# Moving one layer's conditioning dots out of the feed-forward stages and regrouping two feed-forward stages

## The chip, the cores and the metric

The kernel runs on one core of a Trainium2 chip. The metric is the device time of one launch in microseconds (us), the median over runs. A core has five engines that run their own queues: TensorE (PE, matmuls, with PEld for its weight loads), VectorE (DVE), ScalarE (ACT), GpSimd (POOL), and SyncE (SP), which here issues nearly all DMA transfers. They wait for each other through semaphores.

## What is computed

A trunk of two layers over 256 latent tokens and 256 context tokens of width 1024. Every sublayer is normalised, shifted, scaled and gated by vectors that come from a conditioning vector (one for the latent stream, one for the context stream):

```python
for l in range(DEPTH):
    mx = split(silu(c)     @ ada_w[l] + ada_b[l], 9)      # latent stream
    mc = split(silu(c_ctx) @ ada_w[l] + ada_b[l], 9)      # context stream
    x  = x  + mx[2]*0.5*swiglu(modulate(x,  gain[l,0], mx[0], mx[1]), ffn1[l])
    xc = xc + mc[2]*0.5*swiglu(modulate(xc, gain[l,0], mc[0], mc[1]), ffn1[l])
    y_x, y_c = token_mixer(modulate(x, gain[l,1], mx[3], mx[4]),
                           modulate(xc, gain[l,1], mc[3], mc[4]), ...)
    x  = x + mx[5]*y_x
    x  = x + mx[8]*0.5*swiglu(modulate(x, gain[l,2], mx[6], mx[7]), ffn2[l])
    # context likewise, except in the last layer, which drops it after the mixer
return rmsnorm(x) * final_norm
```

`swiglu(h) = (silu(h @ w1) * (h @ w3)) @ w2` with an inner width of 2816, that is 22 tiles of 128. The mixer has three branches (latent attention, differential attention, retention), each gated and summed.

## The kernel before

**Order of the work.** Start-up (norm and the first three inner tiles), FFN (0,0), mixer of layer 0, FFN (0,1), FFN (1,0), mixer of layer 1, FFN (1,1), final norm. PE's instructions stand in the order in which the program writes them; the other engines' instructions and the buffers are ordered by the framework's scheduler, which goes by program order among what it believes to be ready. An order that it has fixed does not change on the chip: an engine waits for the head of its queue.

**Weights.** Every matmul is done in three with a value cut into a high and a low part. `unit` (L193) loads 128 x 1024 weights (512 KB) through SP into one of four `raw` buffers (pool `rawp`), and cuts them in pieces of `PIECE` = 256 columns: ACT copies the high part (`whi`, L206), DVE subtracts it for the low part (`wlo`, L207). Four such cut pairs can exist (pool `wp`). A unit narrower than 1024 is cut in one piece.

**Large tiles.** Pool `qkv` has 16 buffers ("pair") of 512 KB, for inner tiles `g`, the forms `tf`, and all larger tiles of the mixer.

**FFN.** `ffn` (L606) makes the 22 inner tiles in `FF_GROUPS` of 8, 8 and 6. After each group `out_phase` (L404) multiplies them by w2 for 8 output chunks c and adds each chunk into x by DVE (`evac`, L412, two halves of 256 columns). Matmuls of the out phase go chunk by chunk, except that with `nfirst` = 2 the first two chunks go together, inner tile by inner tile. PSUM has three `mm` banks for them.

**Strassen FFNs.** (0,1) and (1,0) make inner tiles in pairs by seven products of half-size blocks instead of eight (`ff_pairs`, L545, `product` of 24 matmuls of 256 columns). The products of a pair come in the order b21, n2, n1, n3, b11 of the next pair (`begin`), n4, b22. `block` (L525) loads a block of weights; with `plus` POOL adds a second one in by an accumulating DMA (W2+W3 for `n`, W0+W2 for `r3`). `cut_weight` (L518) cuts it: ACT L521, then DVE L522. `n` is also added to `r0` (L570), which is then cut for the product n2. One `mm` bank belongs to the pair that has begun, also across an out phase. `token_forms` builds the six `tf` tiles first.

**Conditioning dots.** For a modulation vector m and a chunk k of 128 rows, `ada` (L284) loads 128 x 1024 of `ada_w` (512 KB, tile `araw`, SP L292), and `ada_dot` (L278) multiplies and sums it with silu(c) of each stream on DVE (L281). Each 128-row chunk is a load and one dot for each stream that needs it. `hook(n)` (L309) allows 2n dots more and writes them at that place in the program; `PACE` = (per inner step, per output chunk) sets n. In FFN (0,0) the dots are those of layer 0 (vectors 2 to 8) and of layer 1 (vectors 0 to 2): 80 loads, 160 dots, at PACE (3.2, 1.5). FFN (0,1) has vectors 3 and 4 of layer 1 (16 loads, 32 dots), FFN (1,0) vectors 5 to 8 for the latent stream alone (32 loads, 32 dots), both at one `hook(1.0)` for each chunk of an out phase that is not the last. `cond` (L269) loads c and c_ctx and applies Silu.

**Mixer.** It calls `gemm` (L223) 89 times in layer 0, in this order of what matters here: 8 for differential attention's q and k, 8 for retention and 2 for the latent k/v as fill between the steps of differential attention, then a gate (8 x 3 matmuls) and a projection (4 x 3) alternately for the second and the third branch, with 6 for the latent branch's q and rotary parts in between, then the heads. Every call takes one weight unit or half of one.

## Time and profile before

| what | us |
|---|---|
| median of 3 runs (2298.07 to 2298.66) | 2298.34 |
| the profiled execution's own time | 2294.51 |
| its span, first to last instruction | 2292.6 |
| PE busy | 2207.6 |
| DVE busy | 1621.8 |
| ACT busy | 1058.1 |
| moved by DMA | 345.44 MB, mean 151 GB/s |

The span is the time that the profile shows; the profiled execution's own time is 1.9 us more. PE's busy time is modelled, so a stretch is also judged by how many matmuls of which width it holds against a stretch in which PE never waits. Busy time of the other engines is a union of instructions, and two that follow each other closely overlap by some tens of ns.

### The profile page before, as it was taken

What the parts mean: (1) busy time and instruction counts of PE and PEld (TensorE: products, weight loads), DVE (VectorE), ACT (ScalarE), POOL (GpSimd) and SP (SyncE); (2) the same over time, 40 slices, a digit from 0 to 9 for tenths busy, and PEclk for the clock granted to TensorE, in tenths of its full rate; (3) what the DMA queues carried; (4) which work ended last, traced back from release to release, by engine and by line L of the source; (5) the groups of instructions that cost most, each with busy time, mean ns of one, the idle gap of its engine ahead of it and who ended that gap; (6) DMA issues with size and microseconds to landing.
All of it is one profiled execution on the core that took longest, in us unless ns stands there. A gap on an engine that the chain in (4) does not pass through costs nothing.

```text
span 2292.6 us, 36217 instructions
## 1 busy us (share of the span) xinstructions
PE 2207.6 (96%) x13578; PEld 1933.6 (84%) x13578; DVE 1621.8 (71%) x3604; ACT 1058.1 (46%) x2617; POOL 131.8 (6%) x166
## 2 busy tenths in 40 slices
PE   9989989999999999999999998989999999999998
PEld 6868777887788877898898998888988889989998
DVE  4899998658645455678875776777567786777665
ACT  4413223437533256444353545335354574565554
POOL 2000000000000000000000000000000000110000
PEclk9999999999999999999999999999999999999999
DMA  8567665331213313436764635885452233435553
GB/s 316 193 220 230 228 209 193 122 101 56 74 54 97 94 61 96 140 93 199 219 174 119 176 79 152 268 248 173 127 176 91 96 111 116 152 117 178 185 184 111
DMA packets 98271, 345.44 MB, mean 151 GB/s; under 512 B 11312, under 2 KB 12208, under 8 KB 98096
## 3 DMA queue, kind: packets, MB, share of 16 engines
q1 hardware_dynamic: 89568, 313.76, 41.6%
q0 software_dynamic: 7808, 27.27, 6.1%
q8 instruction: 107, 1.75, 0.3%
q10 hardware_dynamic: 720, 2.11, 0.3%
q14 instruction: 68, 0.56, 0.1%
HBM read 338.89 MB, written 4.19 MB: 150 GB/s over the span
## 4 chain that ended last, share of the span: by engine, by line
PE 60%; DVE 16%; issue 11%; DMA 11%; ACT 2%; POOL 0%; POOLq 0%; DVEq 0%; SPq 0%; ACTq 0%
PE mm L216 15%; PE mm L217 15%; PE mm L218 14%; DVE junk L281 7%; DMA raw<-in_w13p 5%; DMA araw<-in_ada 5%; DVE wlo L522 2%; DVE wlo L207 2%; PE s L216 2%; PE s L217 2%; PE s L218 2%; PE o L211 2%; PE s L211 2%; PE t L211 2%; PE t L912 1%
## 5 line engine op out<-in xcount | busy, mean ns | idle before, releaser
L206 ACT CAST whi<-raw 128x256 fp32r<-128x256 f32 (+1 forms) x1222 | 437.9, 421 | 391.7 <-PE mm L218 139.1
L207 DVE TENSOR_TENSOR wlo<-raw,whi 128x256 fp32r<-128x256 f32 x1214 | 481.8, 440 | 185.0 <-ACT whi L206 183.1
L216 PE MATMUL mm<-h,wlo 128*128 128x256 f32 (+2 forms) x1272 | 435.4, 342 | 0.4 <-DVE wlo L207 0.4
L218 PE MATMUL mm<-h,whi 128*128 128x256 f32 (+2 forms) x1272 | 426.3, 335 | 0.0
L217 PE MATMUL mm<-h,whi 128*128 128x256 f32 (+2 forms) x1272 | 426.0, 335 | 0.0
L216 PE MATMUL mm<-g,wlo 128*128 128x512 f32 (+1 forms) x758 | 269.5, 355 | 25.0 <-DVE wlo L207 20.1
L281 DVE SCALAR_TENSOR_TENSOR junk<-araw,cond 128x1024 bf16<-128x1024 f32 x224 | 271.6, 1218 | 22.7 <-DMA araw<-in_ada 22.3
L217 PE MATMUL mm<-g,whi 128*128 128x512 f32 (+1 forms) x758 | 266.7, 352 | 3.2 <-DVE g L601 1.7
L216 PEld LDWEIGHTS mm<-h,wlo 128*128 128x128 f32 (+1 forms) x1272 | 241.1, 190 | 33.2 <-issue 9.4
L218 PE MATMUL mm<-g,whi 128*128 128x512 f32 (+1 forms) x758 | 265.9, 351 | 0.0
L218 PEld LDWEIGHTS mm<-h,whi 128*128 128x128 f32 (+1 forms) x1272 | 240.9, 189 | 25.4
L217 PEld LDWEIGHTS mm<-h,whi 128*128 128x128 f32 (+1 forms) x1272 | 241.3, 190 | 22.4 <-issue 0.2
L216 PE MATMUL s<-h,wlo 128*128 128x256 f32 (+1 forms) x848 | 259.0, 305 | 0.0
L217 PE MATMUL s<-h,whi 128*128 128x256 f32 (+1 forms) x848 | 258.6, 305 | 0.0
L218 PE MATMUL s<-h,whi 128*128 128x256 f32 (+1 forms) x848 | 258.5, 305 | 0.0
L521 ACT CAST whi<-raw 128x1024 fp32r<-128x1024 f32 x140 | 145.5, 1047 | 162.3 <-DMA raw<-in_w13p 84.4
L522 DVE TENSOR_TENSOR wlo<-raw,whi 128x1024 fp32r<-128x1024 f32 x140 | 170.1, 1220 | 29.0 <-ACT whi L521 29.0
L216 PEld LDWEIGHTS mm<-g,wlo 128*128 128x128 f32 x758 | 144.1, 190 | 52.0 <-DVE wlo L207 19.9
L216 PE MATMUL mm<-tf,wlo 128*128 128x256 f32 x480 | 144.9, 302 | 35.9 <-DVE wlo L522 28.7
L216 PEld LDWEIGHTS s<-h,wlo 128*128 128x128 f32 x848 | 163.4, 193 | 6.8
L217 PEld LDWEIGHTS s<-h,whi 128*128 128x128 f32 x848 | 163.1, 192 | 6.7
L218 PEld LDWEIGHTS s<-h,whi 128*128 128x128 f32 x848 | 162.9, 192 | 6.7
(296 smaller groups left out, 3851.5 us busy)
## 6 DMA issues: line engine op xcount, KB each, us to landing
araw<-in_ada SPq DMA_DIRECT2D x128, 512.0 KB, 4.1
raw<-in_w13p SPq DMA_DIRECT2D x100, 512.0 KB, 3.5
raw<-in_w SPq DMA_DIRECT2D x90, 512.0 KB, 4.3
raw<-in_win SPq DMA_DIRECT2D x90, 512.0 KB, 3.5
raw<-in_w2a SPq DMA_DIRECT2D x64, 512.0 KB, 4.1
raw<-in_w13p POOLq DMA_DIRECT2D x40, 512.0 KB, 6.1
raw<-in_w2c SPq DMA_DIRECT2D x32, 384.0 KB, 3.1
raw<-in_wbr SPq DMA_DIRECT2D x24, 512.0 KB, 3.5
```

What stands on the lines that cost most here:

```text
L206: nc.scalar.copy(hi[:, c], raw[:, c])
L207: eng.tensor_tensor(out=lo[:, c], in0=raw[:, c], in1=hi[:, c].bitcast(F32), op=ALU.subtract)
L211: self.nc.tensor.matmul(out, lhsT=lhsT, rhs=rhs, start=start, stop=stop)
L216: nc.tensor.matmul(out, lhsT=sl, rhs=mh, start=start, stop=False, **kw)
L217: nc.tensor.matmul(out, lhsT=sh, rhs=ml, start=False, stop=False, **kw)
L218: nc.tensor.matmul(out, lhsT=sh, rhs=mh, start=False, stop=stop, **kw)
L281: self.nc.vector.scalar_tensor_tensor(out=junk, in0=raw, scalar=1.0, in1=cond[s], op0=ALU.mult, op1=ALU.mult, accum_out=self.mods[l][:, s, ...
L521: nc.scalar.copy(hi, raw)
L522: nc.vector.tensor_tensor(out=lo, in0=raw, in1=hi.bitcast(F32), op=ALU.subtract)
L912: nc.tensor.transpose(pt[:, b * 128:(b + 1) * 128], P[:, b * 128:(b + 1) * 128], self.ident)
```

## The change

All dots of layer 1 are written into the mixer of layer 0, at 1.8 dots for each `gemm` call (`DOTS` = 0.9), one stream after the other: 9 vectors for the latent stream (72 loads, 72 dots), then 5 for the context stream (40 loads, 40 dots). Each load now takes a `raw` buffer of `rawp`, the one that weights use; silu(c) takes one `qkv` buffer, loaded through POOL. FFN (0,0) keeps the 112 dots of layer 0 at PACE (2.2, 0.9). The Strassen FFNs have no dots, go in groups of 6, 6, 6 and 4 inner tiles with their own layout of w2 (`w2s`, `w2t`, made on the host as the other layouts are), and load `r1` and `n` of the next pair into `qkv` buffers when that pair begins. Groups of 6 start an out phase with two chunks together. Units of 1024 columns are cut in two pieces instead of four.

```diff
-PIECE = 256
+PIECE = 512
-PACE = ((3.2, 1.5), (0.0, 1.0), (0.0, 1.0))
+PACE = ((2.2, 0.9), (0, 0), (0, 0))
+ST_GROUPS = ((0, 6), (6, 12), (12, 18), (18, 22))
+DOTS = 0.9
...
     def gemm(self, out, w, acts, cols, m=128, off=0):
+        if self.mixing:
+            self.hook(DOTS)
...
+    def ada_streams(self, l, streams):
+        nc, a = self.nc, self.a
+        for s, mods in streams:
+            cond = self.qkv.tile([128, 1024], F32, tag="pair", name="cond1")
+            nc.gpsimd.dma_start(cond, a["cvec"][s].to_broadcast([128, 1024]))
+            nc.scalar.activation(cond, cond, AF.Silu)
+            for m in mods:
+                for k in range(KD):
+                    raw = self.rawp.tile([128, 1024], F32, tag="raw", name="araw")
+                    nc.sync.dma_start(raw, a["ada"][l, m, k])
+                    self.ada_dot(l, m, k, raw, {s: cond}, (s,))
+                    if k == KD - 1:
+                        self.ada_done(l, s, m)
+                    yield 1
...
-        nfirst = 2 if gm == 5 or len(halves) == 1 else 0
+        nfirst = 2 if gm == 5 or len(halves) == 1 or len(acts) == 6 else 0
...
-    def block(self, src, plus=None):
-        raw = self.rawp.tile([128, 1024], F32, tag="raw", name="raw")
+    def block(self, src, plus=None, pool=None):
+        if pool is None:
+            raw = self.rawp.tile([128, 1024], F32, tag="raw", name="raw")
+        else:
+            raw = pool.tile([128, 1024], F32, tag="pair", name="raw")
...
-            begun[p] = r0, q1, s1
+            n = self.block(W[p, 2], W[p, 3], pool=self.qkv)
+            r1 = self.block(W[p, 1], pool=self.qkv)
+            begun[p] = r0, r1, n, q1, s1
...
-            r1 = self.block(W[p, 1])
             q2, q3 = self.s_bank(), self.s_bank()
             self.product(q2, self.cut_weight(r1), B["b21"], True, True)
             add(out=s1, in0=s1, in1=q2, op=ALU.add)
             self.gated(s1, g1, HX)
-            n = self.block(W[p, 2], W[p, 3])
+            r3 = self.block(W[p, 0], W[p, 2])
             wn = self.cut_weight(n)
             add(out=r0, in0=r0, in1=n, op=ALU.add)
             self.product(q1, self.cut_weight(r0), B["n2"], False, False)
...
             self.product(q3, wn, B["n1"], True, False)
-            r3 = self.block(W[p, 0], W[p, 2])
+            r4 = self.block(W[p, 3])
...
             if p + 1 < NFF // 2:
                 begin(p + 1)
-            r4 = self.block(W[p, 3])
...
-        self.adaq = itertools.chain(self.ada(0, range(2, NMOD), cond), self.ada(1, range(3), cond))
+        self.adaq = self.ada(0, range(2, NMOD), cond)
...
+            if not last:
+                self.adaq = self.ada_streams(l + 1, ((0, range(NMOD)), (1, range(5))))
+                self.mixing = True
...
-            if not last:
-                self.adaq = self.ada(l + 1, range(3, 5), self.cond(nc.scalar))
-                self.pace = PACE[1]
+            self.run(self.adaq)
+            self.mixing = False
+            self.pace = PACE[1]
...
-                self.run(self.adaq)
-                self.adaq = self.ada(l + 1, range(5, NMOD), self.cond(nc.scalar))
-                self.pace = PACE[2]
```

## Rows read from the trace of the kernel before

**Rows 1.** The page's first part: busy time by engine over the span.
```profile
PE 2207.6 (96%) x13578; PEld 1933.6 (84%) x13578; DVE 1621.8 (71%) x3604; ACT 1058.1 (46%) x2617; POOL 131.8 (6%) x166
```
**Rows 2.** Who PE waited for: total us, times, longest us; the two largest.
```profile
PE mm L216 <- DVE wlo L522: 28.7, 13, 5.1
PE mm L216 <- DVE wlo L207: 20.5, 13, 5.8
```
**Rows 3.** Stretches: from:to, length, busy (instructions) by engine, clock, DMA; FFN (0,0).
```profile
118.30:176.80 58.50, 47.69 (x194) 36.38 (x194) 56.67 (x120) 11.22 (x33) 0.00 (x0) 0.97 0.68 220
176.80:264.50 87.70, 87.32 (x385) 71.82 (x384) 81.17 (x178) 29.29 (x79) 0.00 (x0) 1.00 0.67 220
264.50:322.30 57.80, 47.26 (x193) 36.41 (x193) 55.85 (x121) 11.24 (x33) 0.00 (x0) 0.94 0.70 226
387.60:419.60 32.00, 29.70 (x165) 25.49 (x163) 19.19 (x42) 12.93 (x31) 2.90 (x5) 1.00 0.56 195
```
**Rows 4.** Stretches of the two Strassen FFNs, columns as in the group before.
```profile
1000.00:1066.90 66.90, 62.22 (x492) 61.32 (x491) 47.53 (x71) 37.91 (x68) 3.43 (x4) 0.95 0.61 174
...
1111.80:1206.00 94.20, 84.99 (x674) 84.19 (x673) 72.52 (x116) 49.89 (x85) 5.11 (x6) 0.95 0.68 190
1206.00:1249.50 43.50, 43.50 (x194) 36.03 (x193) 20.46 (x44) 10.53 (x25) 1.70 (x2) 1.00 0.44 122
1249.50:1310.00 60.50, 58.20 (x481) 57.74 (x481) 42.07 (x59) 34.62 (x59) 3.41 (x4) 1.00 0.57 158
1372.00:1445.40 73.40, 67.26 (x519) 66.15 (x519) 52.33 (x77) 41.69 (x75) 3.45 (x4) 0.93 0.57 161
1445.40:1491.30 45.90, 43.86 (x195) 36.02 (x194) 36.98 (x79) 10.51 (x25) 1.70 (x2) 1.00 0.87 284
1491.30:1593.00 101.70, 88.13 (x674) 87.38 (x673) 78.03 (x123) 48.59 (x83) 5.11 (x6) 0.92 0.74 216
```
**Rows 5.** The timeline of an out phase of FFN (0,0): start, us, engine, line, [idle before].
```profile
267.78 8.49 SPq L292 DMA_DIRECT2D araw<-in_ada  x5
277.09 0.33 SPq L197 DMA_DIRECT2D raw<-in_w2a  x1
...
282.07 1.33 ACT L206 CAST whi<-raw 128x256 fp32r<-128x256 f32 x4 [9.04 <-DMA raw<-in_w2a]
...
285.07 1.22 DVE L281 SCALAR_TENSOR_TENSOR junk<-araw,cond 128x1024 bf16<-128x1024 f32 x1
...
286.22 1.22 DVE L281 SCALAR_TENSOR_TENSOR junk<-araw,cond 128x1024 bf16<-128x1024 f32 x1
```
**Rows 6.** Groups by line and shape: count, busy us, mean ns, idle before and its releasers.
```profile
L207 DVE TENSOR_TENSOR wlo<-raw,whi 128x256 fp32r<-128x256 f32 x1168 | 440.3, 422 | 159.0 <-ACT whi L206 157.5
...
L384 DVE TENSOR_TENSOR g<-gg,g 128x512 fp32r<-128x512 f32 x26 | 17.6, 684 | 0.0
...
L412 DVE SCALAR_TENSOR_TENSOR x<-mm,mods,x 128x256 f32<-128x256 f32 x192 | 86.3, 479 | 106.5 <-PE mm L218 106.1
...
L207 DVE TENSOR_TENSOR wlo<-raw,whi 128x768 fp32r<-128x768 f32 x34 | 32.3, 955 | 14.1 <-ACT whi L206 13.9
```
**Rows 7.** The Strassen chain behind one stall without dots: the add of `n`, POOL's DMAs.
```profile
L570 DVE TENSOR_TENSOR raw<-raw 128x1024 f32<-128x1024 f32 x20 | 24.5, 1224 | 62.0 <-DMA raw<-in_w13p 62.0
...
1286.44 0.85 POOL L529 DMA_DIRECT2D raw<-in_w13p  x1 [1.04 <-DMA raw<-in_w13p]
...
1289.89 1.23 DVE L570 TENSOR_TENSOR raw<-raw 128x1024 f32<-128x1024 f32 x1 [4.13 <-DMA raw<-in_w13p]
```
**Rows 8.** Stretches of the mixer of layer 0, columns as in the stretches above.
```profile
450.40:493.90 43.50, 43.50 (x194) 36.02 (x192) 27.08 (x73) 18.24 (x52) 3.67 (x5) 1.00 0.32 101
...
550.00:605.00 55.00, 54.41 (x300) 43.42 (x299) 44.33 (x121) 42.83 (x132) 3.85 (x4) 1.00 0.23 77
...
730.00:805.00 75.00, 75.00 (x329) 61.43 (x328) 38.80 (x85) 26.12 (x71) 8.55 (x11) 1.00 0.32 100
```
**Rows 9.** ScalarE's table loads, grouped by the line that needs them.
```profile
L778 ACT ACT_TABLE_LOAD x2 | 2.6, 1283 | 0.0
```

More of the change, by code (lines that the diff above doesn't have):

```diff
@@ L1 @@
 import heapq
-import itertools
 import math
@@ L282, in ada_dot, with ada_done @@
                                                 accum_out=self.mods[l][:, s, m, k:k + 1])
+    def ada_done(self, l, s, m):
+        nc = self.nc
+        sm, d = self.sm[l], self.mods[l][:, s, m, :]
+        nc.vector.tensor_tensor(out=d, in0=d, in1=sm[:, SM_ADAB + m * KD:SM_ADAB + (m + 1) * KD], op=ALU.add)
+        if m in (1, 4, 7):
+            j = m // 3
+            nc.vector.scalar_tensor_tensor(out=self.gs[l][:, s, j, :], in0=d, scalar=1.0,
+                                           in1=sm[:, SM_GAIN + j * KD:SM_GAIN + (j + 1) * KD],
+                                           op0=ALU.add, op1=ALU.mult)
+        elif m in (2, 5, 8):
+            nc.vector.tensor_scalar_mul(d, d, 0.5)
     def ada(self, l, mods, cond):
         nc, a = self.nc, self.a
-        M, sm = self.mods[l], self.sm[l]
         self.araw = [self.qkv.tile([128, 1024], F32, tag="pair", name="araw") for _ in range(2)]
         for m in mods:
-            ns = (0,) if l == DEPTH - 1 and m > 4 else (0, 1)
             for k in range(KD):
@@ L292, in ada @@
                 nc.sync.dma_start(raw, a["ada"][l, m, k])
-                self.ada_dot(l, m, k, raw, cond, ns)
+                self.ada_dot(l, m, k, raw, cond, (0, 1))
                 if k < KD - 1:
-                    yield len(ns)
-            for s in ns:
-                d = M[:, s, m, :]
-                nc.vector.tensor_tensor(out=d, in0=d, in1=sm[:, SM_ADAB + m * KD:SM_ADAB + (m + 1) * KD], op=ALU.add)
-                if m in (1, 4, 7):
-                    j = m // 3
-                    nc.vector.scalar_tensor_tensor(out=self.gs[l][:, s, j, :], in0=d, scalar=1.0,
-                                                   in1=sm[:, SM_GAIN + j * KD:SM_GAIN + (j + 1) * KD],
-                                                   op0=ALU.add, op1=ALU.mult)
-                elif m in (2, 5, 8):
-                    nc.vector.tensor_scalar_mul(d, d, 0.5)
-            yield len(ns)
+                    yield 2
+            for s in range(2):
+                self.ada_done(l, s, m)
+            yield 2
+    def ada_streams(self, l, streams):
[10 more added lines that the diff above has]
+                    if k == KD - 1:
+                        self.ada_done(l, s, m)
+                    yield 1
     def hook(self, n):
@@ L434, in out_phase @@
                 evac(c, ps, s, hc)
-            if gm != 5 and after is None:
+            if gm != 5 and after is None and self.pace[1]:
                 self.hook(self.pace[1])
@@ L560, in ff_pairs @@
                 begin(p)
-            r0, q1, s1 = begun.pop(p)
+            r0, r1, n, q1, s1 = begun.pop(p)
             g1, g2 = (self.pair("g") for _ in range(2))
-            r1 = self.block(W[p, 1])
             q2, q3 = self.s_bank(), self.s_bank()
@@ L625, in ffn @@
         h = self.hn
-        for gi, (f0, f1) in enumerate(FF_GROUPS):
+        st = (l, i) in STRASSEN
+        groups = ST_GROUPS if st else FF_GROUPS
+        for gi, (f0, f1) in enumerate(groups):
             gts = start
@@ L642, in ffn @@
             ng = f1 - f0
-            w2 = a["w2c"][l, i] if gi == 2 else a["w2a"][l, i, gi]
-            end = gi == len(FF_GROUPS) - 1
+            end = gi == len(groups) - 1
+            if st:
+                j = STRASSEN.index((l, i))
+                w2 = a["w2t"][j] if end else a["w2s"][j, gi]
+            else:
+                w2 = a["w2c"][l, i] if end else a["w2a"][l, i, gi]
             self.out_phase(lambda c: self.unit(w2[c], ng * 128), gts, l, gm, halves,
@@ L1444, in build @@
                        lambda *v: self.start_norm(l, 2, acc2, *v, stash=not last), pre)
-            if not last:
-                self.adaq = self.ada(l + 1, range(3, 5), self.cond(nc.scalar))
-                self.pace = PACE[1]
+            self.run(self.adaq)
+            self.mixing = False
+            self.pace = PACE[1]
             acc = self.tmp("acc")
@@ L1533, in _layout @@
     g["w2c"] = _cols(w2[:, :, 2048:], 128)
+    w2 = np.stack([w2[li] for li in STRASSEN])
+    g["w2s"] = _cols(w2[:, :2304].reshape(len(STRASSEN), 3, 768, D), 128)
+    g["w2t"] = _cols(w2[:, 2304:], 128)
     w = np.stack([g["w13"][li] for li in STRASSEN])
```

## The prediction, made before the changed kernel was built

> **What bounds the kernel now.** I read the page's first part, then who PE waited for, then stretches of one stage each, and in the stretches with idle PE the timeline. PE is the bound: 2207.6 of 2292.6 us [rows 1]. What it waits for is nearly all DVE's low parts of weights, of plain units (L207) and of Strassen blocks (L522) [rows 2]. So the question is where DVE, or what feeds it, is late.
>
> I measure a stage against one in which PE never waits. The out phase at 1206 us has 194 matmuls of 512 columns in 43.5 us, 0.224 us each, with PE busy throughout; in Strassen stretches 481 matmuls of 256 columns keep PE busy for 58.20 us, 0.121 us each [rows 4]. This counts idle time and the slower matmuls after it, where the granted clock reads 0.92 to 0.97.
>
> FFN (0,0): two out phases take 58.5 and 57.8 us against 43.5, so 15.0 and 14.3 us are lost; 0.4 in the inner steps between, 2.3 in the last out phase [rows 3]: 32 us in all. DVE is busy 97% of the first. Why: an output chunk takes 43.5 / 8 = 5.44 us of PE. DVE's work for it at the old pace is 3 dots, four cuts of 0.422 and two evacuations of 0.479 [rows 6]. Dots start 1.15 us apart when they follow each other (285.07 and 286.22) [rows 5]. So 3.45 + 1.69 + 0.96 = 6.10 us, more than PE's. An inner step of 48 x 0.224 = 10.75 us holds 6.4 dots, eight cuts and two 512-wide operations: 7.36 + 3.38 + 1.37 = 12.1 us, more again. And dots hold up weights in SP: five dot loads took 8.49 us to issue, since each waits for a buffer that a dot must free; the w2 load behind them went at 277.09, and ACT stood idle for 9.04 us for it [rows 5].
>
> Strassen: what is lost is length minus 0.121 us per matmul. The stretches at 1000, 1111.8, 1249.5, 1372 and 1491.3 lose 7.4, 12.7, 2.3, 10.6 and 20.2 us; the one at 1636.5 is like that at 1249.5, 2.3; the out phase at 1445.4 loses 45.9 - 195 x 0.224 = 2.2 [rows 4]. Together 57.7; the other out phases lose under 1.5 each, left out. The stretches at 1249.5 and 1636.5 have no dots in them, so they tell what is left without dots: 2.3 us for 2.9 pairs. What they still wait for is `n`: POOL can issue the accumulating part at 1286.44 only, after the first part has landed, and the add that needs it runs at 1289.89 after 4.13 us of idle DVE; over both FFNs these 20 adds follow 62.0 us of DVE idle time [rows 7].
>
> **The change part by part.**
>
> *FFN (0,0).* 48 of 160 dots leave. A cut of a unit in two pieces costs 2 x 0.684 by the nearest row, the 512-wide subtraction of `g` [rows 6]: 1.37 us instead of 1.69. A chunk now needs 1.8 x 1.15 + 1.37 + 0.96 = 4.40 of 5.44 us, an inner step 4.4 x 1.15 + 2.74 + 1.37 = 9.17 of 10.75. DVE has 15 to 19% to spare, so the backlog goes, and with it most of SP's queue. Left are the waits for the last `g` at the start of an out phase; the third now starts two chunks together, which gives it time. I leave 4 of 32 us: gain 28, between 20 (weights still queue behind dot loads now and then) and 30.
>
> *Strassen FFNs.* 64 dots leave, and every pair stretch becomes one without dots. `n` and `r1` are loaded from the time that a pair begins: four products (b11, n4, b22, b21, 4 x 24 x 0.121 = 11.6 us) before n2, instead of when one of four `raw` buffers comes free. That covers two transfers in sequence. For each FFN I leave: 5.1 us at the start (7.4 less one dot-free 2.3, the forms, unchanged); for ten pairs, 3.5 times 2.3 = 8.0 if the buffers bring nothing and 0 if all, I take 4, as DVE still has to cut `n`, add, and cut again in that order; for the out phases 2.3. These have a new wait: with two chunks together and one of three `mm` banks held by the pair that has begun, the third chunk waits for the first one's evacuation, 2 x 0.479 us, while the second chunk's last matmuls take 3 x 0.224: 0.3 us and the signal, 0.5 each in three out phases, and the last phase's wait for `g`, 0.8. The fourth group adds 8 evacuated chunks of 2 x 0.479, 7.7 us of DVE for each FFN, and they lie beside PE: a chunk of a group of 6 takes 18 x 0.224 = 4.03 us of PE, and DVE needs 0.96 for its cut in one piece and 0.96 for its evacuation [rows 6]. Sum 11.4 for each FFN, 22.8 for both: gain 57.7 - 22.8 = 35. Ends: 22 (buffers bring nothing, the bank wait is 1 us) and 46 (no waits in pairs).
>
> *Mixer of layer 0.* 112 dots come in, 1.8 for each of the first 62 `gemm` calls, which run from 450 to about 830 us, and 40 more loads than in all of before. DVE gains 2.07 us for each call and saves 0.32 for each whole unit. From 450.4 to 493.9 (8 calls): 27.1 + 16.6 - 2.6 = 41.1 of 43.5 us. From 550 to 605 (6 calls, softmax and retention masks): 44.3 + 12.4 - 1.9 = 54.8 of 55. From 730 to 805 (19 calls, some 12.5 whole units): 38.8 + 39.3 - 4.0 = 74.1 of 75 [rows 8]. So DVE is filled in three stretches of 173.5 us together, in which PE now loses nearly nothing. DMA is filled as well: from 730 to 805 it moves 100 GB/s x 75 us = 7.5 MB [rows 8]; 34 loads of 0.524 MB make it 25.4 MB, 339 GB/s, while the highest of these stretches is 284 [rows 4]. At 284 the stage would take 14 us longer. Four cut units (some 4 calls of PE's work) stand as a cushion, since no dot is awaited by a matmul; attention's softmax has no such cushion and queues behind dots. The price has no row. Its ends are what FFN (0,0) lost: 0.4 of 87.7 us with DVE 93% busy, and 15.0 of 58.5 with DVE 97% busy and asked for 112% [rows 3]; over 173.5 us 1 and 45 us. A gain is excluded, as there is no wait to remove. Asked for 94 to 100% it is nearer to the first: I take 12.
>
> *ScalarE's tables.* Two Silu of the conditioning vectors now stand between exponentials, so up to four more table loads of 1.283 us [rows 9], 5 us of ACT, which is busy 18.2 of 43.5 and 26.1 of 75 us there [rows 8]: nothing, or 1.3 us each if a softmax waits. The Trainium skill ("ScalarE: Activation LUTs", What ACT_TABLE_LOAD costs) counts some 2.66 us for a switch, as the drain belongs to it, and advises to batch by set, against this change; by it four switches were 10.6 us and, if all came onto the path, the forecast some 11 us later. No row here shows the drain.
>
> *Cuts of 512 elsewhere* (mixer of layer 1, FFN (1,1)): DVE is no bound there; a first piece comes 0.5 us later where PE waits for it, a few times. I take 0, between -3 and +3.
>
> Sum on the profiled execution: 2294.5 - 28 - 35 + 12 = 2243.5 us. The median before is 3.8 us above that execution, so I forecast 2247.
>
> **Rivals.**
>
> *The mixer gives back much* (DVE full, softmax behind dots): 45 us instead of 12, so 2280. For it: 100% in 550 to 605, where steps follow each other through DVE. Against: dots are spread and awaited by nobody until the next stage. 0.17.
>
> *The stalls were not the dots'*: the new buffers are not free early (16 `qkv` buffers, 6 forms, 6 `g`, two for the next pair's `g` and two pairs of blocks are 16), so `n` comes no earlier, and FFN (0,0) keeps 12: gains 22 and 20, 12 lost, so 2268. That is the case in which the change does only part of what it says. 0.16.
>
> *The mixer hides all* and the buffers hide all: 30 + 46 - 1, so 2223. 0.10.
>
> *Slower: dot loads hold up weights in SP in the mixer.* Dot loads and weights now share four buffers and one queue; one hole of 9 us followed five dot loads [rows 5]. 112 loads make 22 such groups. If the cushion fails in 7 of them, 63 us are gone and the change is worth nothing; if it fails in 11, 99 us: 2298 - 63 + 99 = 2334. Against it: a load here is freed by one dot instead of two, and the mixer's DMA is at 0.23 to 0.32 now [rows 8]. 0.05; that it ends just at no change 0.02.
>
> **How the numbers follow.** The forecast (2235 to 2260) has 0.50, the rivals 0.17, 0.16, 0.10, 0.05 and 0.02. A range from 2220 to 2281 holds the first four for the most part and leaves out the rest. Within 0.2% (4.6 us, about what a measurement of this kernel can tell from no change) is 0.02, slower 0.05, faster 0.93.
>
> **What would show it.** The two first out phases of FFN (0,0) at 44 to 46 us. Strassen pairs near 20.5 us, no wait for L522 over 2 us behind the start, and the adds of `n` with little idle time before them. In the mixer DVE above 90% in the three stretches, and PE idle some 12 us, before low parts of weights from 730 on and before softmax results from 550 on. Wrong would be: FFN (0,0) above 50 us in an out phase (then it was not DVE), or mixer idle above 30 us.

## The result and the profile after

The changed kernel takes 2365.02 us (median of four runs, 2364.48 to 2369.98) where the kernel before takes 2298.2 beside it: 1.0296 times as long, 95% interval 1.0279 to 1.0314. The forecast was 2247, the range ended at 2281: the sign was wrong and 118 us were missed. The runs of the experiments below are one execution each unless a median is given.

A stage is read here from the start of the last matmul of the stage before to the start of its own last one (tile names tell which; the norm's small matmuls between stages count with the next), in the profiled execution.

| us | to the end of FFN (0,0) | mixer 0 | FFN (0,1) | FFN (1,0) | mixer 1 | rest | span |
|---|---|---|---|---|---|---|---|
| before | 425.2 | 545.6 | 375.3 | 387.1 | 350.8 | 208.5 | 2292.6 |
| after | 391.6 | 584.9 | 409.9 | 411.7 | 356.4 | 208.3 | 2362.7 |
| difference | -33.6 | +39.3 | +34.6 | +24.6 | +5.6 | -0.2 | +70.1 |
| forecast | -28 | +12 | -35 for both | | 0 | 0 | -51 |

Such a time varies by some 6 us between kernels that have the same text for the stage. The mixer of layer 0 took 582.9 to 588.9 us in nine kernels that share it (after and eight of the runs below), and FFN (1,0) without dots in its old form took 364.6 to 371.2 in three. A smaller difference that rests on one run is not shown by it.

The page of after, first part, and the groups that answer to [rows 1, 6]:
```profile
PE 2226.1 (94%) x13542; PEld 1943.9 (82%) x13542; DVE 1599.7 (68%) x3016; ACT 1012.5 (43%) x1999; POOL 140.0 (6%) x168
...
L285 DVE SCALAR_TENSOR_TENSOR junk<-araw,cond 128x1024 bf16<-128x1024 f32 x224 | 271.6, 1224 | 17.1 <-DMA araw<-in_ada 12.8
...
L543 DVE TENSOR_TENSOR wlo<-raw,whi 128x1024 fp32r<-128x1024 f32 x140 | 171.0, 1222 | 91.5 <-ACT whi L542 91.2
```
PE waited 136.6 us (span less busy) instead of 85.0, and its busy time rose by 18.5 with 36 fewer records, since matmuls after a hole run slower (the last section has the rows). DVE's cuts of Strassen blocks follow 91.5 us of idle time; in before that was 29.0. Who PE waited for, total, times, longest, the answer to [rows 2]:
```profile
PE mm L218 <- DVE wlo L543: 50.9, 12, 6.2
PE s L218 <- DVE wlo L543: 21.9, 14, 8.1
PE mm L218 <- DVE wlo L209: 11.4, 7, 4.0
PE mm L219 <- DVE g L625: 7.5, 5, 2.3
```
The wait that the new buffers were to shorten, for low parts of Strassen blocks, went from 28.7 to 72.8 us. Stretches of after: FFN (0,0)'s first two out phases, the answer to [rows 3], and one pair of FFN (1,0), the answer to [rows 4]:
```profile
117.70:161.20 43.50, 43.50 (x194) 36.02 (x193) 39.81 (x74) 9.66 (x17) 0.00 (x0) 1.00 0.68 224
248.20:291.70 43.50, 43.50 (x193) 36.02 (x192) 39.98 (x76) 9.66 (x17) 0.00 (x0) 1.00 0.66 214
1537.40:1565.00 27.60, 22.15 (x168) 21.74 (x168) 15.41 (x21) 12.26 (x20) 1.70 (x2) 0.89 0.52 134
```
The out phases have no hole and last 43.5 us instead of 58.5 and 57.8. The pair has 168 matmuls of 256 columns, 20.3 us at 0.121, and lasts 27.6.

### The profile page after: what moved, and what is told of

It is laid out like the page before. It is cut to its first block, busy times and chain, and to the rows that moved or that the text cites. A ratio compares the mean times of both kernels' runs of the same rounds, so it can differ in the third digit from the quotient of the medians.

```text
span 2362.7 us, 35088 instructions
## 1 busy us (share of the span) xinstructions
PE 2226.1 (94%) x13542; PEld 1943.9 (82%) x13542; DVE 1599.7 (68%) x3016; ACT 1012.5 (43%) x1999; POOL 140.0 (6%) x168
## 4 chain that ended last, share of the span: by engine, by line
PE 65%; DVE 11%; issue 10%; DMA 9%; ACT 4%; POOL 0%; SPq 0%; POOLq 0%; DVEq 0%; ACTq 0%
PE mm L218 16%; PE mm L219 15%; PE mm L220 15%; DMA raw<-in_w13p 6%; PE s L218 4%; PE s L219 3%; PE s L220 3%; DVE wlo L543 2%; DMA raw<-in_win 2%; DVE junk L285 2%; PE s L213 2%; PE o L213 2%; DMA araw<-in_ada 2%; PE t L213 1%; DVE wlo L209 1%
## 5 line engine op out<-in xcount | busy, mean ns | idle before, releaser
L208 ACT CAST whi<-raw 128x512 fp32r<-128x512 f32 (+3 forms) x622 | 378.7, 644 | 482.7 <-PE mm L220 167.8
L209 DVE TENSOR_TENSOR wlo<-raw,whi 128x512 fp32r<-128x512 f32 (+2 forms) x614 | 428.7, 719 | 149.5 <-ACT whi L208 147.8
L218 PE MATMUL mm<-g,wlo 128*128 128x512 f32 (+1 forms) x746 | 264.7, 355 | 5.3 <-ACT g L624 3.0
L543 DVE TENSOR_TENSOR wlo<-raw,whi 128x1024 fp32r<-128x1024 f32 x140 | 171.0, 1222 | 91.5 <-ACT whi L542 91.2
L433 DVE SCALAR_TENSOR_TENSOR x<-mm,mods,x 128x256 f32<-128x256 f32 x224 | 99.2, 479 | 137.9 <-PE mm L220 137.7
```

Source lines behind the costliest of these rows:

```text
L208: nc.scalar.copy(hi[:, c], raw[:, c])
L209: eng.tensor_tensor(out=lo[:, c], in0=raw[:, c], in1=hi[:, c].bitcast(F32), op=ALU.subtract)
L218: nc.tensor.matmul(out, lhsT=sl, rhs=mh, start=start, stop=False, **kw)
L433: nc.vector.scalar_tensor_tensor(out=self.xT[c][:, hc], in0=ps[:, hc], scalar=self.mods[l][:, s, gm, c:c + 1], in1=self.xT[c][:, hc], op0= ...
L543: nc.vector.tensor_tensor(out=lo, in0=raw, in1=hi.bitcast(F32), op=ALU.subtract)
```

## Experiments: the Strassen FFNs

**Which part.** Three parts touch these stages: the dots that left, the groups of 6, the early loads of `n` and `r1`. The first run takes back the early loads.
```diff
-            n = self.block(W[p, 2], W[p, 3], pool=self.qkv)
-            r1 = self.block(W[p, 1], pool=self.qkv)
             (abridged: r1, n, r3, r4 loaded where the kernel before loads them)
```


> The changed kernel, with the five weight blocks of a Strassen pair loaded where and into what they were loaded before (r1 and n in raw buffers, after the pair has begun); groups of 6, no dots, and all else stay changed. In the changed kernel the two Strassen FFNs take 409.8 and 411.7 us (375.3 and 387.1 before). Theory Q: the loads of n and r1 stand in SP's queue behind the next pair's r3, r4 and r0, so n comes 8 us late in every pair; with the old places both FFNs fall to 355 to 368 us, and the kernel to about 2270 us. Rival G: the fourth group, two chunks at a time on the two banks that are left, or cuts of 768 columns make the FFNs long; then they stay above 395 us and the kernel above 2330 us.

Measured 2290.25 us; FFN (0,1) and (1,0) 370.9 and 376.3, so the early loads cost 39.0 and 35.4 us. The next run also has the old groups, so that the dots alone are taken out of these stages.
```diff
-        groups = ST_GROUPS if st else FF_GROUPS
+        groups = FF_GROUPS
             (abridged: with w2a and w2c as before, no two chunks together)
```


> The changed kernel with the Strassen FFNs entirely as before (blocks, groups of 8, 8 and 6, one chunk at a time), but without dots in them. It measures the dots alone, and against a1 (370.9 and 376.3 us) the groups of 6 alone. Theory of the prediction (without dots 2.3 us are lost in 2.9 pairs, the start 5.1): both FFNs 360 to 367 us, so groups of 6 cost some 8 us each. If groups of 6 are worth something, 372 us or more. Kernel about 2271 us in the first case.

Measured 2274.83 us; 364.1 and 366.2, and mixer 1 at 351.4. Three terms follow from these runs, over both stages: the dots' leaving gains 32.1 (with the w2 units cut in two pieces instead of four), the groups of 6 cost 16.9, and 5.2 more in mixer 1, the early loads cost 74.4; -32.1 + 16.9 + 74.4 is the +59.2 of the table. What the groups cost is seen in the waits of the run with old loads and new groups; the run with the old groups has no wait for `x`:
```profile
PE mm L218 <- DVE wlo L543: 15.3, 11, 3.2
...
PE mm L218 <- DVE x L433: 10.6, 12, 1.8
```
Each of the six out phases has two of these twelve waits. The third chunk waits 0.38 us for a bank, where I had taken 0.5. The eighth waits 1.0 to 1.8 us, which I had not seen: it needs the bank of the sixth chunk, and DVE empties that one late, since it first waits for `n` of the next pair, adds it and cuts. In the first out phase the sixth chunk's matmuls end before 1075, and DVE works in this order:
```profile
1076.22 1.23 DVE L594 TENSOR_TENSOR raw<-raw 128x1024 f32<-128x1024 f32 x1 [4.44 <-DMA raw<-in_w13p]
...
1079.77 0.87 DVE L433 SCALAR_TENSOR_TENSOR x<-mm,mods,x 128x256 f32<-128x256 f32 x2
```
The second cost lies behind the FFNs: 2.5 and 2.4 us pass from the last matmul of each to the first of the next stage, where the old groups have 0.1 and 0.3. One of these stands in FFN (1,0), the other is nearly half of mixer 1's 5.2.

**Is it the order of the loads?** In after, SyncE issues `n` and `r1` of the next pair behind `r3`, `r4` and the next `r0`, and POOL's accumulating DMA (the second part of `n`) follows late. `issue_after` holds the loads in the order written.
```diff
+        with nullcontext() if self.last_load is None else self.tc.issue_after(self.last_load):
+            load = self.nc.sync.dma_start(raw, src).ins
+        if pool is not None:
+            self.last_load = load
```


> The changed kernel, n and r1 still loaded into the large buffers when a pair begins, but the other block loads are held behind them in SP's queue, so that SP's order is the program's (n and r1 of a pair stand ahead of the next pair's r3, r4, r0). Theory Q: it is the order alone, so both FFNs fall to 350 to 368 us and the kernel to about 2265 us. Rival B: early loading is itself the harm (three transfers at once, the accumulating one after them, and large buffers that are full when the first pair begins); then the FFNs stay above 390 us.

Measured 2369.35 us; 411.2 and 413.0. `n` now landed at 1521.4 us, 20 us before n2 started, and PE still waited 3.6 us before n2 at each of the six transitions from pair to pair inside a group, in both FFNs. The order of the loads isn't the cause: the data is there, and the pair is no shorter. DVE's timeline in this run, one pair (start, length, line, operation, idle before):
```profile
1529.05 0.43 DVE L629 TENSOR_TENSOR g<-sw,g 128x256 fp32r<-128x256 f32 x1 [0.47 <-ACT g L628]
1533.20 0.43 DVE L626 TENSOR_TENSOR su<-su 128x256 f32<-128x256 f32 x1 [3.72 <-ACT su L625]
1534.15 1.23 DVE L544 TENSOR_TENSOR wlo<-raw,whi 128x1024 fp32r<-128x1024 f32 x1 [0.52 <-ACT whi L543]
...
1536.22 1.22 DVE L544 TENSOR_TENSOR wlo<-raw,whi 128x1024 fp32r<-128x1024 f32 x1
...
1537.69 1.22 DVE L599 TENSOR_TENSOR raw<-raw 128x1024 f32<-128x1024 f32 x1
...
1540.90 1.22 DVE L544 TENSOR_TENSOR wlo<-raw,whi 128x1024 fp32r<-128x1024 f32 x1
```
DVE stands idle for 3.72 us until `su`, the copy of n4's result, comes from ScalarE. Then the cut of `r1`, the cut of `n`, the add `r0 += n` and the cut of that sum run, with other work between them, until 1542.1, and n2 starts at 1542.17; the products before it had ended at 1538.57. None of these four needs `su`. In the kernel before, where `n` is late, the add of [rows 7] (at 1289.89, behind 4.13 us of idle DVE) is followed by:
```profile
1291.03 1.22 DVE L522 TENSOR_TENSOR wlo<-raw,whi 128x1024 fp32r<-128x1024 f32 x1
1292.17 1.22 DVE L588 TENSOR_TENSOR raw<-raw 128x1024 f32<-128x1024 f32 x1
1293.30 1.22 DVE L522 TENSOR_TENSOR wlo<-raw,whi 128x1024 fp32r<-128x1024 f32 x1
1294.44 0.42 DVE L598 TENSOR_TENSOR su<-su 128x256 f32<-128x256 f32 x1
```
These are the cut of `n`, the add for b22, the cut of the sum, and only then `su`; n2 starts at 1294.58. So in the kernel before, the four microseconds of idle DVE stand before the add, and `su` comes behind the cuts. With early loads they stand before `su`, and the cuts come behind it.

**Moving the cuts in the text.** Two runs write cuts of the next pair at the end of `begin`: `n`, the add and the sum in one, `r1` and `n` in the other, both with loads in order.
```diff
-            begun[p] = r0, r1, n, q1, s1
+            begun[p] = r0, r1, n, self.cut_weight(r1), self.cut_weight(n), q1, s1
```


> The kernel with the loads in order (a2), and in the program the cut of n, the add of n to r0 and the cut of that sum moved up to the end of begin, ahead of the evacuation of n4 and b22. In a2 n had landed 15 us before n2 (1521.4 against 1536), but DVE's queue held the add and the cut behind the evacuations of n4 and b22, which wait for PE, and n2 waited 3.76 us in every pair. Theory O: DVE's fixed order is the cause, with SP's; then these waits go (8 or so for each FFN, 3.8 us each), the 8.3 us at the first pair stay, and the FFNs fall from 411.2 and 413.0 to 372 to 384 us. Rival B: transfers (three at once, then the accumulating one) are too late whatever the order; then they stay above 400 us.

> The kernel with the loads in order (a2), and the cuts of the next pair's r1 and n moved to the end of begin in the program, so that on DVE and ACT they stand ahead of the evacuation of n4 instead of behind it; the add of n and the cut of the sum follow them. Unlike a3 this takes two of the four cut buffers ahead of r4, not three parts of them. Theory O (the fixed order on ACT and DVE: ready cuts stand behind evacuations that wait for PE): the 3.76 us before n2 go in the pairs, the 8.3 us at the first pair stay, the FFNs fall from 411.2 and 413.0 to 372 to 388 us. Rival C (the four cut buffers are what limits, and each order only moves the wait): a wait of 2 to 5 us in every pair before another product, FFNs above 400 us.

Measured 2442.04 us (448.4 and 453.0) and 2447.51 (451.8 and 454.0): both some 40 us worse for each stage than with the loads in order alone, with waits of 5.2 to 6.3 us before n4 in nearly every pair, and waits for weights in the out phases. That left two explanations: the four cut buffers run out when cuts are held (C), or the order on DVE and ScalarE does it (O).

**A fifth cut buffer.** To make room, the base gives up a raw buffer and small temporaries; then a buffer is added, with the change's order and with the early cuts (and the loads in order).
```diff
-        self.wp = mk("wp", 4)
+        self.wp = mk("wp", 5)
```


> The changed kernel with three raw buffers instead of four, two buffers instead of three for gg, PT and junk and one for diag and lamj: it frees 6.5 KB in each partition and is the base for the next two, which differ from it by the cut buffers. Mixers and plain FFNs may get longer and are not read here. The pairs of the Strassen FFNs use three raw buffers (r0, r3, r4) and none of the others; r0 of the next pair needs one more while the old r0 is held. Expected: FFN (0,1) and (1,0) 410 to 425 us each, where the changed kernel has 409.9 and 411.7.

> The same with five cut buffers (whi and wlo) instead of four. Theory C (early n and r1 cannot be used, since four cut buffers are all held and a cut waits for the matmuls of the product that holds the oldest): the wait of some 3.8 us in each pair goes, and FFN (0,1) and (1,0) fall by 20 to 40 us each against the run with four. Theory O (VectorE and ScalarE work through a written order in which something that waits for TensorE stands ahead of the cuts of r1 and n): a fifth buffer leaves that order as it is and the two stages stay within 5 us of the run with four.

> Five cut buffers, loads held in order, and the cuts of r1 and n written at the end of begin, which with four buffers gave 451.8 and 454.0 us. Theory C: the wait that moved to n4 there was that of r4's cut for a buffer; with a fifth it goes, and both stages come to 370 to 395. Theory O: the early order removes the wait before n2 only if the buffers allow it, so it expects the same fall here but none in the run before this one. If both stay above 430, neither the number of cut buffers nor the place of these two cuts is the cause.

Measured 2420.59 (420.1 and 418.3), 2410.82 (414.4 and 415.6) and 2464.9 us (438.3 and 440.4). C falls: the buffer gives 5.7 and 2.7 us where 20 to 40 were due, and the early cuts stay above 430. By what I had written, that also speaks against the place of the two cuts; the timeline of DVE in the last run tells what that sentence overlooked:
```profile
1538.81 0.69 DVE L607 SCALAR_TENSOR_TENSOR sw<-sw,s 128x512 f32<-128x512 f32 x1 [6.76 <-ACT sw L606]
...
1542.68 1.23 DVE L544 TENSOR_TENSOR wlo<-raw,whi 128x1024 fp32r<-128x1024 f32 x1 [1.38 <-ACT whi L543]
1543.82 1.22 DVE L598 TENSOR_TENSOR raw<-raw 128x1024 f32<-128x1024 f32 x1
1544.96 3.49 DVE L544 TENSOR_TENSOR wlo<-raw,whi 128x1024 fp32r<-128x1024 f32 x3
```
`begin` is written behind `sw`, which waits for n3's end at 1538. So the four cuts and the add don't come before a wait for PE; they come in a row behind one, and n4, for which the last of them is meant, starts at 1547.37 instead of 1540.9. The text had moved the cuts ahead of n4's own cut instead of ahead of `su`.

**Which block.** One run each with only `n` or only `r1` loaded early.
```diff
-            r1 = self.block(W[p, 1], pool=self.qkv)      (n alone: r1 at the pair's start)
-            n = self.block(W[p, 2], W[p, 3], pool=self.qkv)   (r1 alone: n behind b21)
```


> The changed kernel, with n loaded in begin as in the change and r1 where the kernel before has it (a raw buffer, at the start of the pair). With both early 409.9 and 411.7 us, with neither 370.9 and 376.3. If n alone brings the loss (its add and two cuts come after each other and it is needed at n2): 395 to 412 each. If r1 alone does (its late arrival at the first pair, its raw buffer taken by qkv): 371 to 385. If they share it: in between, near 390.

> The changed kernel with r1 loaded in begin as in the change, and n where the kernel before has it; the other half of the run with n alone early, which gave 412.5 and 408.8 us. Theory O: r1's cut has no long chain behind it, and the add and the two cuts of n then keep the place they have with late loads: FFN (0,1) and (1,0) come out at 371 to 385. If early r1 does as much harm by itself: 395 to 412.

Measured 2363.7 us (412.5 and 408.8) and 2366.77 (407.8 and 415.3): either block alone brings the whole loss, so my expectation for `r1` failed. The two don't add up, as two independent costs would. With `n` alone PE waits as in the run above, 3.3 to 6.5 us before n2 inside a group (and 9 to 10 us before the first n2). With `r1` alone the waits are others: 2.1 to 2.9 us before n2, 15.2 us in all for banks (`x`) and 13.4 us for `sw`.

**The order held by hand.** At the transitions inside a group the four operations are held ahead of `su`, and so is the cut for b22 of the old pair; loads in order, all else as in the change. These are 6 of the 9 transitions of an FFN (the expectation counts 7 of 10).
```diff
+            w22 = self.cut_weight(r1)
+            if p + 1 in begun and (p + 1) % 3:
+                sums(p + 1)          (cuts of r1 and n, add r0 += n, cut of r0)
+            last = self.last_low
+            with self.tc.issue_after(self.last_cut):
+                nc.scalar.activation(su, q1, AF.Copy, scale=-1.0)
+            with self.tc.issue_after(last):
+                self.gated(su, g2, HX)
```


> The changed kernel with its loads in order, and now inside a group (7 of the 10 transitions between pairs) the cuts of the next pair's r1 and n, the add r0 += n and the cut of that sum are held on VectorE and ScalarE ahead of su, the evacuation of n4, which waits for TensorE. That is the order VectorE has where the loads are late; with early loads they stand behind su. The other three transitions and the start of each FFN stay as they are. Theory O (the order, not the buffers): the wait of about 3.8 us before n2 goes in these 7 transitions, 26 us for each FFN: 385 each (380 to 392), where the run with loads in order had 411.2 and 413.0. Theory D (the early blocks cost something else, DMA rate or memory ports): the order does nothing and both stay above 405.

Measured 2282.52 us, and 2295.71 for the kernel before beside it (one run each); FFN (0,1) and (1,0) 366.1 and 370.5. So the order is the cause: 45.1 and 42.5 us come back against the run with the loads in order. I had expected 385, since I priced a transition at its wait of 3.8 us. Laid side by side, the two runs differ by 6.1 to 7.2 us at each of the six transitions, 41.2 us of the 45.1 and 41.6 of the 42.5: the hole of 3.6, and n2 behind it that lasts 4.3 to 5.3 us instead of 2.9. At the group boundaries, where an out phase stands between the pairs, there was no such hole to remove. With the order held the two stages are 4.8 and 5.8 us shorter than with the loads as before; that is within what the same text varies by, so a gain from the early loads is not shown. DVE's timeline of one pair, and the stretch of that pair:
```profile
1478.17 1.22 DVE L544 TENSOR_TENSOR wlo<-raw,whi 128x1024 fp32r<-128x1024 f32 x1 [1.39 <-ACT whi L543]
1479.31 1.22 DVE L591 TENSOR_TENSOR raw<-raw 128x1024 f32<-128x1024 f32 x1
1480.45 1.22 DVE L544 TENSOR_TENSOR wlo<-raw,whi 128x1024 fp32r<-128x1024 f32 x1
...
1482.72 1.22 DVE L544 TENSOR_TENSOR wlo<-raw,whi 128x1024 fp32r<-128x1024 f32 x1
1483.85 0.42 DVE L640 TENSOR_TENSOR su<-su 128x256 f32<-128x256 f32 x1
```
```profile
1476.34:1496.50 20.16, 20.16 (x170) 20.16 (x169) 15.14 (x20) 12.14 (x19) 1.71 (x2) 1.00 0.62 163
```
The cuts fill the time in which DVE stood idle, and PE runs through the pair without a hole. What stays is a hole of 8.1 us at the start of the FFN, before b21 of the first pair (1014.77). `r1` gets its `qkv` buffer late and lands at 1007.39, but its cut stands on ScalarE behind the last of the token forms, which waits for DVE; with late loads that cut ran ahead of it. It is the same kind of turned order:
```profile
1011.80 0.63 ACT L514 ACTIVATE tf<-stash 128x512 fp32r<-128x512 f32 x1 [1.84 <-DVE stash L531]
1012.34 1.03 ACT L543 CAST whi<-raw 128x1024 fp32r<-128x1024 f32 x1
```

## Experiments: the mixer of layer 0

**What its 39 us are.** Stretches over the whole stage in before and after:
```profile
425.00:971.00 546.00, 543.24 (x2752) 437.74 (x2751) 327.54 (x821) 266.34 (x737) 34.98 (x46) 1.00 0.27 85
```
```profile
391.60:976.50 584.90, 556.70 (x2749) 440.35 (x2748) 443.91 (x920) 258.95 (x594) 43.06 (x48) 0.99 0.54 180
```
PE's idle time goes from 2.8 to 28.2 us, and its busy time grows by 13.5 with the same work: matmuls behind holes are slower (granted clock 0.94 in the worst 60 us, below). Two runs take the dots apart: one loads all blocks but multiplies 16 of 1024 columns, which leaves out most of each sum; the other multiplies the conditioning vector by itself and loads no blocks, which leaves out the weights. The third, on the kernel with the old Strassen stages, leaves out dots and loads, and with them the conditioning of layer 1.
```diff
-                    self.ada_dot(l, m, k, raw, {s: cond}, (s,))
+                    self.ada_dot(l, m, k, raw[:, 0:16], {s: cond[:, 0:16]}, (s,))     (loads only)
+                    self.ada_dot(l, m, k, cond, {s: cond}, (s,))                      (dots only, no load)
```


> The changed kernel, whose dots of layer 1 in the mixer take only the first 16 of 1024 columns: all 112 loads, buffers and waits stay, DVE has about 1 us less for each. This leaves out most of the sum in the modulation vectors of layer 1. The mixer of layer 0 takes 584.9 us in the changed kernel and 545.7 before. Theory D: it is DVE's time; the mixer falls to 548 to 556 us. Rival L: it is the loads, which share four raw buffers and SP's queue with weights; the mixer stays at 575 to 590 us. Both in part: in between.

> The changed kernel without the 112 loads in the mixer: each dot multiplies the buffer of silu(c) by itself, at the full 1024 columns, so DVE's work stays and SP's, the raw buffers' and DMA's share goes. This leaves the weights out of the modulation vectors of layer 1. Theory D (DVE's time): the mixer of layer 0 stays at 575 to 590 us. Rival L (the loads): it falls to 548 to 556 us. With this run and the one with loads alone the two shares can be added and held against 39 us.

> The kernel with the Strassen FFNs as before and without dots (a4), and without any dot or load for layer 1, its modulation vectors filled with a constant; this leaves out the conditioning of layer 1. The mixer of layer 0 took 588.9 us in a4 and 545.6 before. If dots and loads are all of the difference, it falls to 545 to 550 us (loads without dots, 564.2, and dots without loads, 569.2, would then each hold about half); if cutting in two pieces has a share of 5 us, to 550 to 555.

Mixer 0 lasted 564.2 us with loads only, 569.2 with dots only, 547.9 with neither. Taking away the dots' DVE time gains 20.7 us of 584.9, taking away the loads gains 15.7: 36.4 of 39.3, so the two costs nearly add up. Both are in the stretches of after (60 us each; the third of the four holds the longest waits):
```profile
520.00:580.00 60.00, 56.24 (x292) 43.71 (x292) 56.71 (x130) 41.77 (x119) 4.54 (x4) 0.97 0.51 168
...
640.00:700.00 60.00, 58.27 (x259) 47.07 (x258) 48.77 (x87) 17.27 (x31) 1.39 (x1) 0.97 0.76 264
700.00:760.00 60.00, 47.95 (x190) 37.22 (x189) 44.72 (x80) 17.71 (x31) 7.11 (x7) 0.94 0.77 255
760.00:820.00 60.00, 55.12 (x247) 41.99 (x246) 51.18 (x93) 20.56 (x37) 4.02 (x4) 1.00 0.86 284
```
From 520 DVE is full (95%). From 700, where PE idles 12 us, DVE is at 75%, so here I put the loss down to the loads. The timelines of SyncE, DVE and ScalarE ahead of the longest wait of PE (4.0 us, until 733.18, for the low part of `wbr`):
```profile
718.33 5.90 SPq L323 DMA_DIRECT2D araw<-in_ada  x3
725.45 0.33 SPq L199 DMA_DIRECT2D raw<-in_wbr  x1
728.49 2.53 SPq L323 DMA_DIRECT2D araw<-in_ada  x2
```
```profile
721.09 1.23 DVE L285 SCALAR_TENSOR_TENSOR junk<-araw,cond 128x1024 bf16<-128x1024 f32 x1 [0.67 <-ACT cond L319]
...
724.14 1.27 DVE L285 SCALAR_TENSOR_TENSOR junk<-araw,cond 128x1024 bf16<-128x1024 f32 x1
```
```profile
730.26 0.62 ACT L208 CAST whi<-raw 128x512 fp32r<-128x512 f32 x1 [6.58 <-DMA raw<-in_wbr]
```
Three dot loads wait in SyncE for buffers, two of them until a dot frees one. The weight stands behind them, and its own buffer is free only when the dot of 724.14 ends, at 725.41; ScalarE idles 6.58 us for it. It is the pattern of [rows 5], in a place where four buffers serve weights and dots together. These are the first dots of the context stream: the first one starts when ScalarE has applied Silu to that stream's vector (`cond`), so a table load stands in this chain too (below).

**Spacing and piece.** Fewer dots for each `gemm`, and cuts in pieces of 256 as before.
```diff
-DOTS = 0.9
+DOTS = 0.64
-PIECE = 512
+PIECE = 256          (a run of its own, DOTS = 0.9)
```


> The changed kernel with DOTS = 0.64, so that 112 dots spread over 88 of the 89 calls of the mixer instead of the first 62. DVE is asked for 0.6 us less in each call. Theory D (DVE and loads asked for 100% in stretches): the mixer of layer 0 falls from 584.9 to 565 to 575 us. Rival R (each dot in front of a softmax or a weight costs the same wherever it stands, and the buffer of silu(c) is held longer where all 16 large buffers are wanted): 583 us or more.

> The changed kernel with PIECE = 256, so units of 1024 columns are cut in four pieces as before. The mixer of layer 1 has no other change and takes 356.4 us instead of 350.8. Theory P: the later first piece costs it; the mixer of layer 1 goes back to 350 to 352 us, that of layer 0 from 584.9 to 578 to 582. If it is something else (a different order of the queues), both stay within 1.5 us.

Mixer 0 lasted 580.7 and 580.0 us, 4.2 and 4.9 below after, and 2 to 3 us below the shortest of the nine kernels with the same mixer. Each rests on one run, so a small gain is likely and its size open. DVE's cuts of plain units in after and in the run with pieces of 256 (count, busy us, mean ns, idle before):
```profile
L209 DVE TENSOR_TENSOR wlo<-raw,whi 128x512 fp32r<-128x512 f32 x536 | 357.1, 689 | 118.0 <-ACT whi L208 117.4
```
```profile
L209 DVE TENSOR_TENSOR wlo<-raw,whi 128x256 fp32r<-128x256 f32 x1040 | 389.4, 422 | 97.6 <-ACT whi L208 96.2
```
Pieces of 512 save 32 us of DVE over the kernel, and yet the stage was no shorter with them. My reading, which no run takes apart, is that PE waits longer for a weight: the first half comes after 0.69 instead of 0.42 us, and ScalarE's high part ahead of it is longer too. The Trainium skill ("VectorE: DVE Perf Modes", The TRN2 errata) advises tiles of 512 elements and more, as each instruction pays a fixed latency; the rows agree on DVE's busy time. A second pair of runs, below, also has the shorter mixer with the smaller piece (568.5 against 572.4). In the run with pieces of 256 throughout, FFN (0,1) fell from 409.9 to 404.2 and mixer 1 stayed at 356.9, so its +5.6 isn't the piece; it goes with the groups (350.8 to 352.2 in five kernels with the old ones, 355.4 and more in all with the new).

**A version that beats both.** The old Strassen stages, and 16 of the 112 dots of layer 1 back in FFN (0,0), both streams of one vector for one load, which has room; then pieces of 512 in FFN (0,0) only.
```diff
-PACE = ((2.2, 0.9), (0, 0), (0, 0))
+PACE = ((2.5, 1.05), (0, 0), (0, 0))
-DOTS = 0.9
+DOTS = 0.75
+        self.adaq = itertools.chain(self.ada(0, range(2, NMOD), cond), self.ada(1, range(1), cond))
+            self.piece = 256      (behind FFN (0,0); the second run alone)
```


> A version meant to beat both: Strassen FFNs as before without dots (a4), vector 0 of layer 1 back into FFN (0,0) for both streams at once (8 loads, 16 dots, PACE (2.5, 1.05)), the other 96 dots in the mixer at DOTS = 0.75. DVE in FFN (0,0) is asked for 5 x 1.15 + 2.74 + 1.37 = 9.9 of 10.75 us in an inner step, so it should stay within 3 us of 393. The mixer at 0.35 us a dot falls from 588.9 by 6, by up to 10 with the lower rate. Kernel 2263 to 2270 us against 2274.8 of a4; if FFN (0,0) loses more than 8 us, no gain.

> The same version with cuts of 256 columns from the mixer of layer 0 on (512 in FFN (0,0)). With 256 throughout, the changed kernel's mixer took 580.0 instead of 584.9 us and its FFN (0,1) 404.2 instead of 409.9. If that was the cut size, 5 to 10 us below the version with 512 throughout, 2255 to 2265 us; otherwise the same within 3 us.

Measured 2260.7 and 2256.21 us (median of four, 2254.68 to 2257.39); the second is 0.9796 times the kernel before (0.9777 to 0.9816). FFN (0,0) kept its gain (393.0 and 392.1 to its end), mixer 0 came to 572.4 and 568.5. The step to 2260.7 from the old Strassen stages alone (2274.83) changes where dots stand and how they are spaced at once, so neither has a price of its own. Its page begins:
```profile
PE 2197.5 (97%) x13578; PEld 1928.3 (85%) x13578; DVE 1610.5 (71%) x3488; ACT 1049.5 (47%) x2503; POOL 135.2 (6%) x168
```

## Why the prediction was wrong, step by step

**What bounds the kernel, FFN (0,0): right.** The stage gained 33.6 where 28 (20 to 30) was forecast, and the out phases came to 43.5, not 44 to 46. DVE's load went as reckoned, from 56.67 us busy in 58.5 to 39.81 in 43.5. From the first out phase to the end of the second, ScalarE waited 60.7 us for weight loads before and nothing after, though dot loads still waited in SyncE for dots (93.7 us in all). No run parts DVE's time from the queue of loads here.

**Strassen, dots: right.** The dots-free stretch as a measure held: the two stages without dots, and with nothing else changed but the piece, lasted 364.1 and 366.2 us, a gain of 32.1.

**Strassen, early loads: the step that failed.** I costed `n` and `r1` from "four products cover two transfers", and took 4 us for each FFN between 0 and 8, that is, a gain with no loss possible. That bounded the load and not the order in which DVE then works. [rows 7] showed the add with DVE waiting 4.13 us for `n`; I read it as a price of late data. In that order `su` came behind the cuts, which was a good place for them. With `n` and `r1` early, DVE's order has `su` first and the cuts behind it: 39.0 and 35.4 us lost in the two FFNs, in place of the 4 us that I had left. The 8.1 us at the start of each FFN are of the same kind, on ScalarE. The rival "not free early" was half true of after's loads and not the cause: with the data 20 us early the stages were no shorter.

**Strassen, groups of 6: mis-sized.** 0.5 us for each bank wait of the third chunk and 0.8 for the last `g` stood in the sum; the stages lost 6.8 and 10.1 us to the groups (one run each, so the split is rough), and mixer 1, costed at 0, another 5.2. The third chunk's wait was right, at 0.38 us. Missing were the eighth chunk's, 1.0 to 1.8 us, and the 2.5 and 2.4 us before the next stage.

**Mixer 0: direction right, size wrong.** 12 stood in the sum, bounds 1 and 45; it was 39.3. I chose the value nearer to the row with DVE at 93%, from DVE alone, and named DMA's 14 us without putting them in. The runs give some 21 us for DVE and 16 for the loads; the latter is close to those 14, but that is luck, as far as the rows tell: PE idled most at 255 GB/s, and 5 us at 284, so the loads seem to act by waiting for buffers in SyncE rather than by the rate. The rival at 45 was nearer, and the pattern of the slower rival (weights behind dot loads) was there, at 16 of its 99 us.

**ScalarE's tables: small, and not isolated.** The stage has 5 table loads of 1.28 us, 3 more than before. None is named as the end of a wait of PE. But the one below stands in the chain ahead of PE's longest wait of the stage, since the first dot of the context stream starts when this Silu is done (721.09 above); what it costs PE there no run shows. The rows show 1.28 us and the next activation at once:
```profile
718.71 1.28 ACT L319 ACT_TABLE_LOAD   x1
720.00 1.06 ACT L319 ACTIVATE cond<-cond 128x1024 f32<-128x1024 f32 x1
```
The Trainium skill ("ScalarE: Activation LUTs", What ACT_TABLE_LOAD costs) counts some 2.66 us for a switch with a drain; the activation ahead of this one ended as the load began, so the trace shows 1.29 us from load to activation and no drain beside it.

**What stays open.** Why the order of VectorE turns when loads come earlier was not tried; that the loss goes when the order is held is shown. With `r1` alone early the loss is as large, but with waits in other places, and which order brings them was not followed up. Whether early loads are worth anything with the order held (some 5 us for each FFN, on one run) is not shown, and that together with the split dots and the old groups was not run.

## What to carry to other kernels

An earlier load can turn the order of the engine that uses it: before costing it as a gain, list what the engine does between the wait that goes and the next wait for PE, and ask which of it will now stand behind that second wait. Idle time in front of an operation that waits for data can be the cheap place for it. A hole of the bounding engine is to be priced with the slower work behind it: here 6 to 7 us for a hole of 3.6. Where work moves into a stage that is free of waits, price the engine and the load queue separately and add them: they nearly added up here, 21 and 16 us.

## What was not expected of the hardware

A hole of PE costs more than its length. The product n2 of 24 matmuls takes 2.88 us in a pair without holes, and 4.28 to 5.29 behind the twelve holes of 3.6 us with the loads in order, by the starts of the products in the trace. Two stretches over n2 with the loads in order, and one with the order held; the number behind the engines' busy times is the granted clock:
```profile
1459.47:1464.76 5.29, 5.29 (x25) 5.29 (x25) 2.89 (x4) 0.42 (x2) 0.00 (x0) 0.50 0.49 149
1542.17:1546.45 4.28, 4.28 (x25) 4.28 (x26) 2.88 (x4) 0.42 (x2) 0.21 (x1) 0.65 0.65 194
```
```profile
1484.98:1487.86 2.88, 2.88 (x26) 2.88 (x25) 1.29 (x4) 1.91 (x4) 0.00 (x0) 1.00 0.48 175
```
The first n2 ran at the lower of the two levels, 1.2 GHz, throughout; the second for part of it; the third at 2.4 GHz. Before the first two PE had waited 3.6 us, before the third not at all. In n2 alone that is 1.4 or 2.4 us on top of the hole. A shorter hole can do it too: with the loads as before PE waited 1.80 us until 1505.07, and n2 took 4.44 us at a granted clock of 0.62. Not every hole does: in after one of 3.61 us, until 1646.31, left n2 at 2.97 us. Over the whole kernel PE's busy time rose by 18.5 us with no more matmuls.
